# Attention rounds in another order: VectorE's steps at fixed places, the reciprocal in quarters, GpSimd's sum in two buffers

## The chip, the cores and the metric

The kernel runs on one core of one Trainium2 chip. The metric is the device time of one execution in microseconds; of the kernel before there are three runs beside the profiled one. Short names are those of the profile: PE is TensorE's matrix multiplication, PEld its loading of weights, DVE is VectorE, ACT is ScalarE, POOL is GpSimd, SP is SyncE, which issues the DMAs.

## What is computed

The reference is a trunk of two layers over 1,024 latent and 256 context tokens, each 1,024 wide. The first layer is a state-space mixer, the second an attention mixer; a last norm closes it. The change lies in the attention of the second layer alone, which computes, for 16 query heads that share 4 key heads:

```python
def attend(q, k, v):
    bsz, lq = q.shape[:2]
    q = q.reshape(bsz, lq, A_NKV, A_REP, A_HEADDIM)
    s = jnp.einsum('bqgrd,bkgd->bgrqk', q, k).astype(F32) * (A_HEADDIM ** -0.5)
    p = jax.nn.softmax(s, axis=-1).astype(v.dtype)
    o = jnp.einsum('bgrqk,bkgd->bqgrd', p, v)
    return o.reshape(bsz, lq, A_W)
...
    o_lat = (ol * jax.nn.silu(gl)) @ out_w
```

Only the latent tokens' output is wanted, over 1,280 keys (context and latent) and 1,024 queries.

## The kernel before, in words

**Units.** The attention stage works on 16 units, u = 0 to 15: a pair of heads times one half (512) of the queries. A unit goes over the ten key tiles of 128 keys, kt = 0 to 9. Its softmax needs a shift per query, and this comes from a pass of its own, the *maxima*: an approximate product of queries and keys (queries on the partitions, high parts alone), of which VectorE takes the largest along the keys. The maxima of unit u+2 are made while unit u and the beginning of u+1 are worked on.

**Rounds.** PE works in rounds, two key tiles to a round, so a unit has five (L1651 to L1682). In a round stand

- two *scores* steps, S0 and S1 (L1658 to L1664): each is 8 matmuls of three products of high and low parts and a row that adds the shift, into a pair of PSUM banks with tag "sc";
- two *maxima* steps, M0 and M1 (`maxima`, L1594 to L1622, and `max_tile`, L1457 to L1463): each is one tile of queries against 512 keys, or two against 256 (the rows with 128x256), also into a pair of "sc";
- one *values* step, V (L1674 to L1680): 4 matmuls of the two key tiles of the round before with their values, summed in the bank "ot" over the unit.

There are three pairs "sc", handed out in the order in which PE's steps stand; a step gets the pair of the step three before it, and so waits until that one has been read: a scores step by ScalarE's exponential (L1668, into a tile P), a maxima step by VectorE's maximum along the free axis (L1609).

**Sums.** The softmax's divisor is the sum of the ten P tiles. GpSimd adds tiles 0, 1, 2, 3, 5, 6 and 8 (SUM_POOL, L30), VectorE 4, 7 and 9 (`add_up`, L1635 to L1647; the first add of either takes two tiles). VectorE then joins both sums (L1688), and PE sums over the partitions, the *divisors* step D (L1698 to L1701), which ends a unit. ScalarE copies the result (L1705), VectorE takes the reciprocal (L1709), GpSimd multiplies it by the gate (L1710), VectorE multiplies the unit's output by that (L1711), into `at`. A small turn of the maxima (T, L1618) stands in the round after D.

**A block** is what lies between two D steps: five rounds of M and S and V, one T, one D. In a block, rounds 1 to 3 hold the scores of kt 4 to 9 of a unit, rounds 4 and 5 those of kt 0 to 3 of the next; all ten maxima tiles of a later unit; VectorE's adds and join of the unit; and the reciprocal, gate product and output product of the unit whose D came just before. There are 14 blocks with maxima, of which 13 have the reciprocal of a unit before them. Then two units follow without maxima.

**The order.** A planner (`Plan`, L52 to L131) lays all steps out by rank, by estimated durations and by what they need, and emits them; each engine then runs its own list strictly in that order, waiting on semaphores. PE's list is fixed: `pe` (L1579) gives every step a place, a number 5u + round + fraction, and the steps are chained in the order of these numbers (L1721). The other engines' lists come from the planner, which takes 1.3 us for an add on VectorE, 2.8 us for one on GpSimd, 3.35 us for the reciprocal.

Of the kernel before, what the change touches and what calls it, by code (L numbers as in the profile page):

```python
# [8 lines left out]
FT = mybir.dt.float32  # L9
# [3 lines left out]
OP = mybir.AluOpType  # L13
# [132 lines left out]
def emit(tc, A, out):  # L146
# [834 lines left out]
    with ExitStack() as st:  # L981
# [265 lines left out]
        tabs = []  # L1247
# [310 lines left out]
    with ExitStack() as st:  # L1558
# [7 lines left out]
            return psum("sc", [128, 2, 512])  # L1566

        NP, NU = 6, len(units)
        plan = Plan({"q": 3, "sc": 3, "ot": 1, "dn": 1, "P": NP, "accP": 1, "accV": 1, "mx": 2, "rb": 2, "sg": 2, "ob": 2, "wr": 4})
        qs3.append([S4.tile([128, 512], FR, name=f"q2{i}") for i in range(3)])  # L1570
        at = [S4.tile([128, 8, 512], FT, name=f"at{i}") for i in range(2)]
        setup = plan.op("POOL", lambda: empty_rows(qs3[2]), [], -1000, .6)
# [6 lines left out]
        def pe(when, *args, **kw):  # L1579

            turns.append((when, len(turns), plan.op("PE", *args, **kw)))
            return turns[-1][2]

        def queries(u):
            held[u] = plan.hold("q")
# [8 lines left out]
        def maxima(u):  # L1594

            x, q, R = qs3[u % 3], held[u], 100 * u - 130
            hm, t, rs = plan.hold("mx"), {}, []
            for i in range(10):
                hs = plan.hold("sc")

                def scores(i=i):
                    t[i] = pair()
                    max_tile([t[i][:, h] for h in range(2)], u, x, i)

                def reduce(i=i):
                    if not i:
                        t["m"] = max_tiles(u)
                    o = t[i].rearrange("p h (q k) -> p h q k", q=2) if i % 5 == 4 else t[i]
                    V.tensor_reduce(max_place(t["m"][0], i), o, AX.X, OP.max)  # L1609

                a = pe(5 * u - 8 + i // 2 + (.2, .4)[i % 2], scores, [brought[u]], R, .24, takes=[hs], uses=[q], table="rows")
                rs.append(plan.op("DVE", reduce, [a], R + 10 * i - 60, 1.22, takes=[] if i else [hm], uses=[hs, hm]))
            a = plan.op("DVE", lambda: largest(t["m"][1], t["m"][0]), rs, R + 30, .25, uses=[hm])
            hs = plan.hold("dn")

            def turn():
                t["p"] = psum("dn", [128, 512])[0:64, 0:128]
                T.transpose(t["p"], t["m"][1], ident)  # L1618

            a = pe(5 * u - 3 + .52, turn, [a], R, .12, takes=[hs], uses=[hm], table="cols")  # L1620
            a = plan.op("ACT", lambda: S.activation(t["m"][2], t["p"][0:8], AF.Copy), [a], R - 100, .27, uses=[hm, hs])
            shifts[u] = plan.op("SP", lambda: shift_row(x, t["m"][2]), [a], R - 100, .8, uses=[hm, q], small=True)  # L1622

        def unit(u):
            b, p = units[u]
            kv, R, t = p // 2, 100 * u, {}
            x, q = qs3[u % 3], held[u]
            ho, hg, ha = plan.hold("ot"), plan.hold("sg"), {e: plan.hold("acc" + e[0] if e == "POOL" else "accV") for e in ("POOL", "DVE")}
            sums = {"POOL": [], "DVE": []}

            def gate():
                t["g"] = S4.tile([128, 512], FT, tag="sg", bufs=2, name="sg")
                Q.dma_start(t["g"], sg_d[p, :, b * 512:(b + 1) * 512])

            def add_up(*tiles, e, rank):  # L1635

                if len(tiles) == 1:
                    return
                E, (k0, e0, h0), (kt, e1, h1), two = G if e == "POOL" else V, tiles[0], tiles[-1], len(tiles) == 2

                def add():
                    if two:
                        t[e] = S4.tile([128, 1024], FT, tag="acc" + e, bufs=1, name="acc")
                    E.tensor_tensor(t[e], t["P", k0] if two else t[e], t["P", kt], op=OP.add)  # L1644

                t["a" + e] = plan.op(e, add, [e1, e0 if two else t["a" + e]], rank, 2.8 if e == "POOL" else 1.3,
                                     takes=[ha[e]] if two else [], uses=[ha[e], h1] + ([h0] if two else []))  # L1647

            g = plan.op("SP", gate, [], R, takes=[hg])
            pv = None  # L1650
            for j in range(5):  # L1651
                kts = (2 * j, 2 * j + 1)
                hp = [plan.hold("P") for _ in kts]
                es = []
                for i, kt in enumerate(kts):
                    hs = plan.hold("sc")

                    def scores(kt=kt):  # L1658
                        o = t["s", kt] = pair()
                        k = slice(kt * 128, (kt + 1) * 128)  # L1660
                        for n in range(4):
                            for h, r in enumerate(HALF):
                                T.matmul(o[:, h], (first_row[r] if n == 3 else (kh, kl, kh)[n][r, kv, k]), x[(0, 0, 1, 2)[n]][r],  # L1663
                                         start=(n == 0), stop=(n == 3))  # L1664

                    def expo(kt=kt):
                        t["P", kt] = p_tile()
                        S.activation(t["P", kt], flat(t["s", kt]), AF.Exp)  # L1668

                    a = pe(5 * u + j + (.1, .3)[i], scores, [brought[u], shifts[u]], R, .95, takes=[hs], uses=[q], table="rows")  # L1670
                    last_scores[:] = [a]
                    es.append(plan.op("ACT", expo, [a], R + 10 * kt, 1.05, takes=[hp[i]], uses=[hs]))

                def values(kts=kts):  # L1674
                    if not kts[0]:
                        t["o"] = psum("ot", [128, 512])
                    for kt in kts:
                        for h in range(2):
                            T.matmul(t["o"][h * 64:(h + 1) * 64], vv[:, kt, kv], t["P", kt][:, h * 512:(h + 1) * 512],  # L1679
                                     start=(kt == 0), stop=(kt == NT - 1))  # L1680

                pv = pe(5 * u + j + 1.5, values, es + [pv], R, 1.72, takes=[] if j else [ho], uses=[ho] + hp, table="cols")  # L1682
                for i, kt in enumerate(kts):
                    e = "POOL" if kt in SUM_POOL else "DVE"
                    sums[e].append((kt, es[i], hp[i]))
                    add_up(*sums[e], e=e, rank=R + 10 * kt + 10)
            hd, hb, he = plan.hold("dn"), plan.hold("rb"), plan.hold("ob")
            a = plan.op("DVE", lambda: V.tensor_tensor(t["DVE"], t["DVE"], t["POOL"], op=OP.add), [t["aPOOL"], t["aDVE"]], R + 110, 1.3,  # L1688
                        uses=list(ha.values()))

            def out_of():
                t["b"] = S4.tile([128, 512], FT, tag="ob", bufs=2, name="ob")
                S.activation(t["b"], t["o"], AF.Copy)

            ev = plan.op("ACT", out_of, [pv], R + 60, .6, takes=[he], uses=[ho])


            def divisors():  # L1698
                t["d"] = psum("dn", [128, 512])
                for h in range(2):  # L1700
                    T.matmul(t["d"][h * 64:(h + 1) * 64], ones[:, 0:64], t["DVE"][:, h * 512:(h + 1) * 512], start=True, stop=True)  # L1701

            def keep():
                t["r"] = S4.tile([128, 512], FT, tag="rb", bufs=2, name="rb")
                S.activation(t["r"], t["d"], AF.Copy)  # L1705

            a = pe(5 * u + (6.6 if u < NU - 1 else 5.6), divisors, [a], R, .87, takes=[hd], uses=[ha["DVE"]], table="cols")
            a = plan.op("ACT", keep, [a], R + 30, .6, takes=[hb], uses=[hd])
            a = plan.op("DVE", lambda: V.reciprocal(t["r"], t["r"]), [a], R + 90, 3.35, uses=[hb])  # L1709
            a = plan.op("POOL", lambda: G.tensor_tensor(t["r"], t["r"], t["g"], op=OP.mult), [a, g], R + 90, 1.4, uses=[hb, hg])  # L1710
            finished[u] = plan.op("DVE", lambda: V.tensor_tensor(at[b][:, p], t["b"], t["r"], op=OP.mult), [a, ev], R + 90, .66,  # L1711
                                  uses=[hb, he])

        for u in range(NU):
            queries(u)
# [2 lines left out]
        for u in range(NU):  # L1718
            unit(u)

        turns.sort(key=lambda x: x[:2])  # L1721
        for x, y in zip(turns, turns[1:]):
            y[2].after.append(x[2])


        wparts, X4 = {}, {}
# [29 lines left out]

        def table(i, src):
            def bring():
                tabs[i] = S4.tile([128, 1024], FT, tag="acc" + ("POOL", "DVE")[i], bufs=1, name="tab")
# [140 lines left out]
```

## Time and profile before

| what | value |
|---|---|
| median of three runs | 2016.39 us (2014.74 to 2016.62) |
| profiled execution: its time, its span | 2017.43 us, 2015.7 us |
| granted TensorE clock, mean | 0.993 |
| scores steps (L1663), first and last start | 1523.0 us, 1905.4 us |
| busy over the whole span: PE, DVE, ACT, POOL | 97%, 71%, 56%, 59% |

The span runs from the first instruction to the last; the rest of a run's time lies around it. The stage that the change touches is about 387 us of it, a fifth. A share of busy time over the whole span says little here, since the state-space layer before and the output product behind it have other limits; the stage has to be looked at by its own window, and inside it by its rounds, which repeat.

### The profile page before, as it was taken

How to read it: one execution, taken by the hardware profiler on the slowest of the kernel's cores; microseconds unless marked ns; L12 is line 12 of the kernel's file. 1: busy time of each engine (PE TensorE's matmuls, PEld its weight loads, DVE VectorE, ACT ScalarE, POOL GpSimd, SP SyncE). 2: the span in 40 equal slices, each digit the busy share in tenths (PEclk: the TensorE clock that was granted, in tenths of full speed). 3: DMA queues.
4: the chain of work that ended last, by engine and by line, in shares of the span. 5: the costliest groups of instructions: out<-in, count | busy, mean ns of one | idle time of the engine just before them, and what ended most of it. 6: DMA issues, size and time to landing. Idle time of an engine off the chain costs nothing.

```text
span 2015.7 us, 30716 instructions
## 1 busy us (share of the span) xinstructions
PE 1953.1 (97%) x10728; PEld 1498.7 (74%) x10728; DVE 1433.2 (71%) x1737; ACT 1119.5 (56%) x2047; POOL 1189.5 (59%) x973
## 2 busy tenths in 40 slices
PE   8899999999999999999999999999999999999998
PEld 8778888888888788888878878887775444444476
DVE  1475897786959686866545888767675888888643
ACT  2446767666766677676734776543224445454521
POOL 1211776666846576856459787754265667776722
PEclk9989999999999999999999999999999999999999
DMA  6114463635373545455486675462233111111033
GB/s 243 63 32 119 133 188 113 187 98 163 113 198 92 150 131 162 142 142 158 147 280 215 216 252 191 156 179 93 76 91 93 32 38 48 43 43 37 6 104 105
DMA packets 163151, 255.51 MB, mean 127 GB/s; under 512 B 22490, under 2 KB 58202, under 8 KB 162996
## 3 DMA queue, kind: packets, MB, share of 16 engines
q1 hardware_dynamic: 161844, 251.71, 41.2%
q8 instruction: 84, 1.38, 0.3%
q10 hardware_dynamic: 1152, 1.84, 0.2%
q14 instruction: 71, 0.58, 0.1%
HBM read 210.78 MB, written 42.63 MB: 126 GB/s over the span
## 4 chain that ended last, share of the span: by engine, by line
PE 73%; DVE 8%; DMA 7%; POOL 3%; ACT 3%; issue 3%; SPq 2%; DVEq 0%; POOLq 0%; ACTq 0%
PE pj L168 8%; PE pj L169 7%; PE pj L170 7%; PE sc L1663 7%; PE ot L1679 7%; PE ob L168 6%; PE ob L170 6%; PE ob L169 6%; DVE acc L645 3%; PE sc L1462 2%; PE yo L837 2%; PE st L718 2%; DMA spare<-in_mod_w 2%; DMA es<-e_d 2%; PE sc L168 1%
## 5 line engine op out<-in xcount | busy, mean ns | idle before, releaser
L168 PE MATMUL pj<-inh,whi 128*128 128x512 f32 (+1 forms) x1152 | 442.0, 384 | 3.1 <-DVE dv L453 2.4
L169 PE MATMUL pj<-inl,whi 128*128 128x512 f32 (+1 forms) x1152 | 410.2, 356 | 0.8 <-POOL inl L367 0.8
L170 PE MATMUL pj<-inh,wlo 128*128 128x512 f32 (+1 forms) x1152 | 411.0, 357 | 0.0
L168 PEld LDWEIGHTS pj<-inh,whi 128*128 128x128 f32 x1152 | 219.2, 190 | 31.4 <-DVE dv L453 2.8
L170 PEld LDWEIGHTS pj<-inh,wlo 128*128 128x128 f32 x1152 | 218.5, 190 | 32.3
L645 DVE SCALAR_TENSOR_TENSOR acc<-ub,convw,acc 128x1282 f32<-128x1282 f32 x128 | 229.4, 1793 | 17.0 <-ACT acc L642 14.0
L169 PEld LDWEIGHTS pj<-inl,whi 128*128 128x128 f32 x1152 | 219.6, 191 | 26.6 <-POOL inl L367 1.2
L760 ACT ACTIVATE W<-lab,u_t 128x128 f32<-128x128 f32 x640 | 202.7, 391 | 64.6 <-POOL lab L754 42.0
L754 POOL TENSOR_SCALAR_AFFINE_SELECT lab<-lab 128x512 f32<-128x512 f32 x160 | 145.6, 915 | 153.5 <-DMA lab<-la_d 108.6
L1644 POOL TENSOR_TENSOR acc<-acc,P 128x1024 f32<-128x1024 f32 x80 | 192.8, 2411 | 64.1 <-ACT P L1668 62.6
L1668 ACT ACTIVATE P<-sc 128x1024 f32<-128x1024 f32 x160 | 162.9, 1025 | 120.0 <-PE sc L1663 104.4
L1609 DVE TENSOR_REDUCE mx<-sc 128x2 f32<-128x1024 f32 (+1 forms) x140 | 167.4, 1213 | 37.3 <-PE sc L1462 36.4
L713 POOL TENSOR_TENSOR xw<-xst,te_t 128x256 f32<-128x256 f32 x144 | 143.0, 1009 | 41.6 <-PE st L718 17.5
L1679 PE MATMUL ot<-P,vv 128*64 128x512 f32 x640 | 154.7, 605 | 0.0
L602 POOL TENSOR_TENSOR wlo<-wraw,whi 128x512 fp32r<-128x512 f32 x48 | 72.1, 1501 | 121.9 <-ACT whi L599 121.7
L1663 PE MATMUL sc<-q,kh 64*128 64x512 f32 x640 | 136.6, 423 | 4.9 <-DVE qs L1375 2.6
L1663 PEld LDWEIGHTS sc<-q,kh 64*128 64x128 f32 x640 | 60.4, 185 | 74.6 <-DVE mx L1609 29.6
L170 PE MATMUL ob<-whi,yl 128*128 128x512 f32 x288 | 113.4, 394 | 1.8 <-DVE yl L1061 1.4
L168 PE MATMUL ob<-whi,yh 128*128 128x512 f32 x288 | 113.9, 395 | 0.0
L169 PE MATMUL ob<-wlo,yh 128*128 128x512 f32 x288 | 113.0, 392 | 0.0
L902 DVE SCALAR_TENSOR_TENSOR macc<-mraw,cc,macc 128x512 f32<-128x512 f32 x98 | 101.2, 1058 | 11.1 <-DMA mraw<-in_mod_w 10.9
L732 POOL TENSOR_TENSOR tm<-PV,dec_t 128x512 f32<-128x512 f32 x64 | 92.5, 1446 | 17.8 <-DVE PV L736 16.7
(281 smaller groups left out, 4501.8 us busy)
## 6 DMA issues: line engine op xcount, KB each, us to landing
lab<-la_d SPq DMA_DIRECT2D x160, 256.0 KB
wraw<-in_w_in SPq DMA_DIRECT2D x96, 256.0 KB
workvv<-in_m_out_w SPq DMA_DIRECT2D x94, 256.0 KB
mraw<-in_mod_w SPq DMA_DIRECT2D x64, 256.0 KB
es<-e_d SPq DMA_DIRECT2D x128, 128.0 KB
wraw<-in_wqkv SPq DMA_DIRECT2D x48, 256.0 KB
spare<-in_mod_w SPq DMA_DIRECT2D x32, 256.0 KB
q_d<-qs SPq DMA_DIRECT2D x128, 64.0 KB
```

The costliest lines, as they stand in the source:

```text
L168: T.matmul(o, lh, rh, start=first, stop=False)
L169: T.matmul(o, lh, rl, start=False, stop=False)
L170: T.matmul(o, ll, rh, start=False, stop=last)
L645: V.scalar_tensor_tensor(t["a"], ub[i % 2][:, k:k + CW], convw[:, ct, k:k + 1], t["a"], op0=OP.mult, op1=OP.add)
L713: G.tensor_tensor(t[d], s["xst"][:, c], te_t[:, d, c, h4][:, :, None].to_broadcast([128, 4, 64]), op=OP.mult)
L754: G.affine_select(t["l", d], t["l", d], [[0, 4], [sgn, 128]], OP.is_ge, NEVER, base=0, channel_multiplier=-sgn)
L760: S.activation(t["w", d][:, h], t["l", d][:, h], AF.Exp, bias=u_t[:, d, c, 4 * g + h:4 * g + h + 1])
L1609: V.tensor_reduce(max_place(t["m"][0], i), o, AX.X, OP.max)
L1644: E.tensor_tensor(t[e], t["P", k0] if two else t[e], t["P", kt], op=OP.add)
L1663: T.matmul(o[:, h], (first_row[r] if n == 3 else (kh, kl, kh)[n][r, kv, k]), x[(0, 0, 1, 2)[n]][r], start=(n == 0), stop=(n == 3))
L1668: S.activation(t["P", kt], flat(t["s", kt]), AF.Exp)
L1679: T.matmul(t["o"][h * 64:(h + 1) * 64], vv[:, kt, kv], t["P", kt][:, h * 512:(h + 1) * 512], start=(kt == 0), stop=(kt == NT - 1))
```

## The change

It does four things, all in the attention stage.

1. PE's fixed places: a maxima step with even i moves from .2 to .05 of its round, ahead of the first scores step (.1). A round is M0, S0, S1, M1, V where it was S0, M0, S1, M1, V.
2. VectorE's steps get fixed places too (`dve`), in the same numbering: the maximum of M0 at .1, that of M1 at .5, an add at .75, the join at 5.7, the reciprocal's pieces at 7.3, 7.31, 7.7 and 8.3, the output product at 9.3, the last small maximum at 5u - 3.3. All of them are chained in that order.
3. The reciprocal of 128x512 becomes four of 128x128.
4. GpSimd's running sum gets two buffers instead of one (ring accP), so its first add of the next unit need not wait for VectorE's join. The two tables that later use these buffers follow suit.

```diff
-        plan = Plan({"q": 3, ..., "P": NP, "accP": 1, "accV": 1, ...})
+        plan = Plan({"q": 3, ..., "P": NP, "accP": 2, "accV": 1, ...})
...
+        steps = []
+
+        def dve(when, f, after, rank, us, **kw):
+
+            steps.append((when, len(steps), plan.op("DVE", f, after, rank, us, **kw)))
+            return steps[-1][2]
...
-                a = pe(5 * u - 8 + i // 2 + (.2, .4)[i % 2], scores, [brought[u]], R, .24, ...)
-                rs.append(plan.op("DVE", reduce, [a], R + 10 * i - 60, 1.22, ...))
+                a = pe(5 * u - 8 + i // 2 + (.05, .4)[i % 2], scores, [brought[u]], R, .24, ...)
+                rs.append(dve(5 * u - 8 + i // 2 + (.1, .5)[i % 2], reduce, [a], R + 10 * i - 60, 1.22, ...))
...
-                        t[e] = S4.tile([128, 1024], FT, tag="acc" + e, bufs=1, name="acc")
+                        t[e] = S4.tile([128, 1024], FT, tag="acc" + e, bufs={"POOL": 2, "DVE": 1}[e], name="acc")
...
+                t["a" + e] = plan.op(e, *args, **kw) if e == "POOL" else dve(5 * u + kt // 2 + .75, *args, **kw)
...
+            a = dve(5 * u + 5.7, lambda: V.tensor_tensor(t["DVE"], t["DVE"], t["POOL"], op=OP.add), ...)
...
-            a = plan.op("DVE", lambda: V.reciprocal(t["r"], t["r"]), [a], R + 90, 3.35, uses=[hb])
+            for i in range(4):
+                a = dve(5 * u + (7.3, 7.31, 7.7, 8.3)[i], lambda k=slice(i * 128, (i + 1) * 128): V.reciprocal(t["r"][:, k], t["r"][:, k]),
+                        [a], R + 90, .84, uses=[hb])
...
+            finished[u] = dve(5 * u + 9.3, lambda: V.tensor_tensor(at[b][:, p], t["b"], t["r"], op=OP.mult), ...)
...
-        turns.sort(key=lambda x: x[:2])
-        for x, y in zip(turns, turns[1:]):
-            y[2].after.append(x[2])
+        for order in (turns, steps):
+            order.sort(key=lambda x: x[:2])
+            for x, y in zip(order, order[1:]):
+                y[2].after.append(x[2])
```

**PE, from one round to the next.** In the third block, before the change: the end of S1 (its row of shifts), M1, V, then S0 of the next round in four rows, its M0, and the begin of S1. Here sc is the pair of banks, q the queries, ot the output, vv the values.

```order
L1663 MATMUL sc<-q,first_row 128x512 x2
L1462 MATMUL sc<-kh,q_15402 128x512 x2
L1679 MATMUL ot<-P,vv 64x512 x4
L1663 MATMUL sc<-q,kh 128x512 x2
L1663 MATMUL sc<-q,kl 128x512 x2
L1663 MATMUL sc<-q,kh 128x512 x2
L1663 MATMUL sc<-q,first_row 128x512 x2
L1462 MATMUL sc<-kh,q_15402 128x256 x4
L1663 MATMUL sc<-q,kh 128x512 x2
```

The same place after the change:

```order
L1672 MATMUL sc<-q,first_row 128x512 x2
L1462 MATMUL sc<-kh,q_15402 128x512 x2
L1688 MATMUL ot<-P,vv 64x512 x4
L1462 MATMUL sc<-kh,q_15402 128x256 x4
L1672 MATMUL sc<-q,kh 128x512 x2
L1672 MATMUL sc<-q,kl 128x512 x2
L1672 MATMUL sc<-q,kh 128x512 x2
L1672 MATMUL sc<-q,first_row 128x512 x2
L1672 MATMUL sc<-q,kh 128x512 x2
```

M0 (the row 128x256) has moved ahead of S0, and S1 follows S0 at once. So the pair of M0 now goes to M1 of the same round, with two scores steps between; before, M0's pair went to S0 of the next round, with S1, M1 and V between.

**VectorE, one block.** Before the change, in the middle of the stage: mx are the maxima, rb the reciprocal, at the output product, acc the sum of P tiles (acc<-P its first add, acc<-acc the join), nm the last small maximum.

```order
L1709 RECIPROCAL rb<-rb 128x512
L1609 TENSOR_REDUCE mx<-sc 128x2 x4
L1711 TENSOR_TENSOR at_15405<-ob,rb 128x512
L1644 TENSOR_TENSOR acc<-P 128x1024
L1609 TENSOR_REDUCE mx<-sc 128x2x2
L1609 TENSOR_REDUCE mx<-sc 128x2
L1644 TENSOR_TENSOR acc<-acc,P 128x1024
L1609 TENSOR_REDUCE mx<-sc 128x2
L1688 TENSOR_TENSOR acc<-acc 128x1024
L1609 TENSOR_REDUCE mx<-sc 128x2 x2
L1609 TENSOR_REDUCE mx<-sc 128x2x2
L1477 TENSOR_REDUCE nm_10308<-mx 128x8
```

After the change, the same block from its second piece of the reciprocal on (a maximum and two pieces stand before it):

```order
L1616 TENSOR_REDUCE mx<-sc 128x2
L1720 RECIPROCAL rb<-rb 128x128
L1616 TENSOR_REDUCE mx<-sc 128x2
L1720 RECIPROCAL rb<-rb 128x128
L1616 TENSOR_REDUCE mx<-sc 128x2
L1652 TENSOR_TENSOR acc<-P 128x1024
L1616 TENSOR_REDUCE mx<-sc 128x2x2
L1723 TENSOR_TENSOR at_15405<-ob,rb 128x512
L1616 TENSOR_REDUCE mx<-sc 128x2
L1652 TENSOR_TENSOR acc<-acc,P 128x1024
L1616 TENSOR_REDUCE mx<-sc 128x2 x2
L1697 TENSOR_TENSOR acc<-acc 128x1024
```

The output product has moved behind the first add and behind the maximum of round 3; each add stands right before the maximum of the next round's M0.

**GpSimd, one block.** Before the change: acc<-P is the first add of a unit, rb<-rb,sg the gate product, wol a part of the output weights.

```order
L1644 TENSOR_TENSOR acc<-P 128x1024
L1644 TENSOR_TENSOR acc<-acc,P 128x1024 x3
L1710 TENSOR_TENSOR rb<-rb,sg 128x512
L1644 TENSOR_TENSOR acc<-acc,P 128x1024
L1751 TENSOR_TENSOR wol<-wr,woh 128x512
L1644 TENSOR_TENSOR acc<-acc,P 128x1024
```

After the change:

```order
L1652 TENSOR_TENSOR acc<-P 128x1024
L1652 TENSOR_TENSOR acc<-acc,P 128x1024 x4
L1722 TENSOR_TENSOR rb<-rb,sg 128x512
L1652 TENSOR_TENSOR acc<-acc,P 128x1024
L1764 TENSOR_TENSOR wol<-wr,woh 128x512
```

The gate product now stands behind the add of kt 6 and right before that of kt 8; before, it stood ahead of the add of kt 6.

More of the change, by code (lines that the diff above doesn't have):

```diff
@@ L1568, in emit @@
         NP, NU = 6, len(units)
-        plan = Plan({"q": 3, "sc": 3, "ot": 1, "dn": 1, "P": NP, "accP": 1, "accV": 1, "mx": 2, "rb": 2, "sg": 2, "ob": 2, "wr": 4})
+        plan = Plan({"q": 3, "sc": 3, "ot": 1, "dn": 1, "P": NP, "accP": 2, "accV": 1, "mx": 2, "rb": 2, "sg": 2, "ob": 2, "wr": 4})
         qs3.append([S4.tile([128, 512], FR, name=f"q2{i}") for i in range(3)])
@@ L1609, in reduce @@
                     V.tensor_reduce(max_place(t["m"][0], i), o, AX.X, OP.max)
-                a = pe(5 * u - 8 + i // 2 + (.2, .4)[i % 2], scores, [brought[u]], R, .24, takes=[hs], uses=[q], table="rows")
-                rs.append(plan.op("DVE", reduce, [a], R + 10 * i - 60, 1.22, takes=[] if i else [hm], uses=[hs, hm]))
-            a = plan.op("DVE", lambda: largest(t["m"][1], t["m"][0]), rs, R + 30, .25, uses=[hm])
+                a = pe(5 * u - 8 + i // 2 + (.05, .4)[i % 2], scores, [brought[u]], R, .24, takes=[hs], uses=[q], table="rows")
+                rs.append(dve(5 * u - 8 + i // 2 + (.1, .5)[i % 2], reduce, [a], R + 10 * i - 60, 1.22, takes=[] if i else [hm],
+                              uses=[hs, hm]))
+            a = dve(5 * u - 3.3, lambda: largest(t["m"][1], t["m"][0]), rs, R + 30, .25, uses=[hm])
             hs = plan.hold("dn")
@@ L1642, in add @@
                     if two:
-                        t[e] = S4.tile([128, 1024], FT, tag="acc" + e, bufs=1, name="acc")
+                        t[e] = S4.tile([128, 1024], FT, tag="acc" + e, bufs={"POOL": 2, "DVE": 1}[e], name="acc")
                     E.tensor_tensor(t[e], t["P", k0] if two else t[e], t["P", kt], op=OP.add)
-                t["a" + e] = plan.op(e, add, [e1, e0 if two else t["a" + e]], rank, 2.8 if e == "POOL" else 1.3,
-                                     takes=[ha[e]] if two else [], uses=[ha[e], h1] + ([h0] if two else []))
+                args = add, [e1, e0 if two else t["a" + e]], rank, 2.8 if e == "POOL" else 1.3
+                kw = dict(takes=[ha[e]] if two else [], uses=[ha[e], h1] + ([h0] if two else []))
+                t["a" + e] = plan.op(e, *args, **kw) if e == "POOL" else dve(5 * u + kt // 2 + .75, *args, **kw)
             g = plan.op("SP", gate, [], R, takes=[hg])
@@ L1687, in unit @@
             hd, hb, he = plan.hold("dn"), plan.hold("rb"), plan.hold("ob")
-            a = plan.op("DVE", lambda: V.tensor_tensor(t["DVE"], t["DVE"], t["POOL"], op=OP.add), [t["aPOOL"], t["aDVE"]], R + 110, 1.3,
-                        uses=list(ha.values()))
+            a = dve(5 * u + 5.7, lambda: V.tensor_tensor(t["DVE"], t["DVE"], t["POOL"], op=OP.add), [t["aPOOL"], t["aDVE"]], R + 110, 1.3,
+                    uses=list(ha.values()))
             def out_of():
@@ L1708, in unit @@
             a = plan.op("ACT", keep, [a], R + 30, .6, takes=[hb], uses=[hd])
-            a = plan.op("DVE", lambda: V.reciprocal(t["r"], t["r"]), [a], R + 90, 3.35, uses=[hb])
+            for i in range(4):
+                a = dve(5 * u + (7.3, 7.31, 7.7, 8.3)[i], lambda k=slice(i * 128, (i + 1) * 128): V.reciprocal(t["r"][:, k], t["r"][:, k]),
+                        [a], R + 90, .84, uses=[hb])
             a = plan.op("POOL", lambda: G.tensor_tensor(t["r"], t["r"], t["g"], op=OP.mult), [a, g], R + 90, 1.4, uses=[hb, hg])
-            finished[u] = plan.op("DVE", lambda: V.tensor_tensor(at[b][:, p], t["b"], t["r"], op=OP.mult), [a, ev], R + 90, .66,
-                                  uses=[hb, he])
+            finished[u] = dve(5 * u + 9.3, lambda: V.tensor_tensor(at[b][:, p], t["b"], t["r"], op=OP.mult), [a, ev], R + 90, .66,
+                              uses=[hb, he])
         for u in range(NU):
@@ L1758, in bring @@
             def bring():
-                tabs[i] = S4.tile([128, 1024], FT, tag="acc" + ("POOL", "DVE")[i], bufs=1, name="tab")
+                tabs[i] = S4.tile([128, 1024], FT, tag="acc" + ("POOL", "DVE")[i], bufs=2 - i, name="tab")
                 Q.dma_start(tabs[i], rows(src, 128))
```

## Prediction

> **What bounds the kernel now.** I first read the window of the attention stage's even part, then the chain of waits inside it, round by round, then the waits and groups of VectorE and GpSimd there.
>
> ```profile
> span 2015.7 us, 30716 instructions
> ```
> ```profile
> 1600.00:1850.00 250.00, 248.29 (x1522) 121.75 (x1524) 211.10 (x164) 123.98 (x141) 174.45 (x81) 1.00 0.13 41
> ```
>
> The columns of the window's row are its length, then busy time (and instructions) of PE, PEld, DVE, ACT and POOL, the granted clock, and the DMAs' share. PE is busy for 248.3 of 250 us, VectorE for 211.1 (84%), GpSimd for 174.5 (70%), and DMAs (0.13) bound nothing: the chain should run through PE. It does:
>
> ```profile
> 1654.58 1.13 PE sc L1663 x8
> 1655.70 0.23 PE sc L1462 x2
> 1655.93 0.92 PE sc L1663 x8
> 1656.85 0.03 issue
> 1656.88 0.49 PE sc L1462 x2
> 1657.38 1.87 PE ot L1679 x8
> 1659.24 0.23 PE dn L1618
> ...
> 1662.06 0.23 PE sc L1462 x2
> 1662.29 1.87 PE ot L1679 x8
> 1664.15 1.12 PE sc L1663 x8
> 1665.28 0.23 PE sc L1462 x4
> 1665.51 0.93 PE sc L1663 x8
> 1666.44 0.02 issue
> 1666.46 0.50 PE sc L1462 x2
> 1666.96 1.87 PE ot L1679 x8
> ```
>
> Start, us, what: a round of S0, M0, S1, a short wait, M1, V. In the last five steps, 1664.15 to 1668.83, it takes 4.68 us. Two things stand out. A maxima step costs 0.23, but 0.50 when it starts after a wait; without a wait (1662.06) it is 0.23 and V follows at once. So the wait before M1 costs 0.02 + 0.27 us a round, though PE looks busy. And the first step after V costs some 0.19 more (S0 1.12 against 0.92). Who is waited for:
>
> ```profile
> PEld sc L1462 <- ACT P L1668: 20.7, 51, 0.5
> POOL acc L1644 <- DVE acc L1688: 29.0, 8, 3.9
> ```
>
> These are total, times and longest, in the same 250 us: 51 times in some 51 rounds M1 waits for the exponential that frees its pair. GpSimd's wait for VectorE's join is the one that the second buffer removes; nobody on the path waits for GpSimd there.
>
> The blocks are alike; the last V of a block's round 1, twelve blocks apart:
>
> ```profile
> 1559.31 1.87 PE ot L1679 x8
> ...
> 1853.49 1.87 PE ot L1679 x8
> ```
>
> (1853.49 - 1559.31) / 12 = 24.51 us a block. That is the quantity to forecast; 13 blocks hold a reciprocal.
>
> **PE's new order, if nobody is late.** M1 now takes the pair of M0, so it waits for VectorE instead of ScalarE. S0 takes S1's pair of the round before, long read. A round is then M0 0.23 + 0.19 (first after V), S0 and S1 0.92 each, M1 0.23, V 1.87: 4.36, or 0.32 less than 4.68. Five rounds save 1.6, and a block is 22.9 us. Over 13 or 14 blocks that is 21 to 23 us of gain. It is a ceiling: M1 starts 2.26 after the end of the V before, M0 ends 0.42 after it, and VectorE's maximum has to fit between.
>
> **What VectorE needs.** Rows of it and of its neighbours in the same part:
>
> ```profile
> 1655.26 3.35 DVE L1709 RECIPROCAL rb<-rb 128x512 f32<-128x512 f32 x1 [1.93 <-ACT rb L1705]
> 1658.53 3.58 DVE L1609 TENSOR_REDUCE mx<-sc 128x2 f32<-128x1024 f32 x3
> 1662.33 1.23 DVE L1609 TENSOR_REDUCE mx<-sc 128x2 f32<-128x1024 f32 x1 [0.23 <-PE sc L1462]
> 1663.47 1.33 DVE L1711 TENSOR_TENSOR at<-ob,rb 128x512 f32<-128x512 f32 x1
> 1664.72 2.32 DVE L1644 TENSOR_TENSOR acc<-P 128x1024 f32<-128x1024 f32 x1
> ```
> ```profile
> 1661.87 2.38 POOL L1644 TENSOR_TENSOR acc<-acc,P 128x1024 f32<-128x1024 f32 x1 [0.20 <-ACT P L1668]
> 1664.19 1.76 POOL L1751 TENSOR_TENSOR wol<-wr,woh 128x512 fp32r<-128x512 f32 x1
> ```
> ```profile
> L1688 DVE TENSOR_TENSOR acc<-acc 128x1024 f32<-128x1024 f32 x10 | 12.1, 1211 | 0.2
> L1477 DVE TENSOR_REDUCE nm<-mx 128x8 f32<-128x24 f32 x11 | 2.0, 178 | 0.4
> ```
>
> A maximum takes 1.22 and the next instruction starts 1.14 after it (1662.33, 1663.47). It begins 0.04 after its maxima step's end. An undisturbed add takes 1.21 (the join, L1688).
>
> Now the rows that decide. VectorE's output product starts at 1663.47 while GpSimd adds until 1664.25; it ends at 1664.80, 0.55 after that. Its next add starts at 1664.72 while GpSimd subtracts until 1665.95; it ends at 1667.04, 1.09 after that. An operation of VectorE with two tiles in SBUF does not proceed until GpSimd's running one is done. The reciprocal (one input) and the maxima (from PSUM) are not held. GpSimd in turn: its 1.76 from 1664.19 holds VectorE's 0.55, so a VectorE operation that is already waiting goes first. The opposite case, where GpSimd's next operation is queued and VectorE still waits for a result of GpSimd's:
>
> ```profile
> 1922.95 1.74 POOL L1710 TENSOR_TENSOR rb<-rb,sg 128x512 f32<-128x512 f32 x1
> 1924.65 1.29 POOL L1751 TENSOR_TENSOR klw<-wr,khw 128x512 fp32r<-128x512 f32 x1
> ```
> ```profile
> 1924.72 1.77 DVE L1711 TENSOR_TENSOR at<-ob,rb 128x512 f32<-128x512 f32 x1 [1.18 <-POOL rb L1710]
> ```
>
> The gate product ends at 1924.69, GpSimd's next starts at once, and the output product (1924.72) waits until 1925.94 and ends 0.55 later. After the change the output product stands in just this situation, with an add of 2.37 behind the gate product.
>
> **A block laid out by these rows** (us from the end of the D before; R is a piece of the reciprocal, mx the maximum of the step named). A quarter: 3.35 is 0.15 fixed (the 0.178 of nm less its 24 elements at 1.14 us per 1,024) and 3.20 for 512 columns, so 0.95, and the next starts 0.87 after it. Bounds: 0.84 (a plain quarter) to 1.02 (0.84 and a whole nm). ScalarE's times:
>
> ```profile
> 1654.62 0.60 ACT L1705 ACTIVATE rb<-dn 128x512 f32<-128x512 f32 x1 [2.18 <-PE dn L1701]
> 1655.80 2.11 ACT L1668 ACTIVATE P<-sc 128x1024 f32<-128x1024 f32 x2 [0.58 <-PE sc L1663]
> ```
> ```profile
> 1658.06 2.37 POOL L1644 TENSOR_TENSOR acc<-acc,P 128x1024 f32<-128x1024 f32 x1 [1.80 <-ACT P L1668]
> ```
>
> An exponential starts 0.10 after its scores end (1655.70), two take 2.11, and GpSimd's add starts 0.15 after its tile (1657.91).
>
> - Round 1 (0 to 4.36): mx M0 0.47 to 1.69, in time for M1 at 2.26. R 1.61, R 2.48, mx M1 3.35, R 4.49.
> - Round 2 (T, then 4.59 to 8.95): mx M0 5.36 to 6.58; M1 at 6.85 is safe by 0.2. R 6.50, mx M1 7.37, and the add of kt 4 and 7 asks at 8.51. GpSimd took kt 6 at 7.20 and holds it until 9.57. So the add ends at 10.65.
> - Round 3 (from 8.95): mx M0 only 10.57 to 11.79. M1, due at 11.21, starts at 11.85: 0.64 late, and 0.27 for starting after a wait. V ends at 14.22. The gate product, held by that add, ends at 11.80; kt 8 follows from 11.76 to 14.13. The output product asks at 11.8, ends at 14.68. Then mx M1 14.60 to 15.82, the add of kt 9 to 16.95, and the next mx.
> - Round 4 (from 14.22): S1, due at 15.56, needs M1's pair and starts at 15.88, 0.32 late and 0.2 for the new start. mx M0 16.87 to 18.09, so M1, due at 17.00, starts at 18.15: 1.15 late, and 0.27. V ends at 20.52. The second buffer lets GpSimd's first add of the next unit start when its tiles are there, 18.28 to 20.65; the join, asking at 19.84, ends at 21.73. Before, GpSimd waited for the join.
> - Round 5 (from 20.52): mx M0 21.65 to 22.87; M1, due at 22.78, 0.15 late and 0.27. V ends at 25.30, D (0.86) at 26.16.
>
> The lateness adds up to 0.91 + 0.52 + 1.42 + 0.42 = 3.27, on 22.9: 26.16, which is 1.65 us more than 24.51. The next block begins with VectorE idle, so it repeats. The first block has no reciprocal; there the join asks within 0.1 us of GpSimd's add, so it may gain or lose 1.3, taken as nothing. Units without maxima: the quarters' extra 0.2 lies under PE's other work. SP's loads move by a row; at a DMA share of 0.13 they cost nothing.
>
> **Sum.** 13 x 1.65 = +21.4 us, made against the span of 2015.7 (the profiled execution took 2017.4 in all, the median of three runs is 2016.4). Put on the median: **2038 us**.
>
> [...]
>
> **Rivals.**
>
> *VectorE keeps up* (no add is ever held). Speaks for it: the join took 1.21 in every block before. Against: the first add took 2.32 above. Every block 22.9: 14 x -1.6, 1994 us. 7%.
>
> *Only kt 6 holds an add*: the output product gets in ahead of kt 8, and the join ahead of GpSimd's first add. Round 3 loses 0.91, a block is 23.8; 14 x -0.7, 2006 us. The point is whether VectorE sees the gate product's end before GpSimd takes up kt 8; the rows at 1924.7 say no. 14%. Something between this and my forecast, about as before: 5%.
>
> *The output product first, the rest held.* It ends at 12.45, mx M1 at 13.62; kt 8 runs to 14.65 and holds the add of kt 9 until 15.73; M1 of round 4 is 0.45 late and the join still loses (18.6 against 17.8), which makes M1 of round 5 0.85 late. Block 25.6, +1.1: 2031 us. 14%.
>
> *PE's clock falls in the new pauses.* In the stage it is granted in full (1.00). After a pause of 2.38 us it was not:
>
> ```profile
> 1912.38 0.50 PE L170 MATMUL sc<-woh,P 128*128 128x512 f32 x1 [2.38 <-DVE P L1778]
> ```
> ```profile
> 1910.00:1920.00 10.00, 6.68 (x17) 3.78 (x17) 10.00 (x8) 3.15 (x6) 3.47 (x2) 0.67 0.35 121
> ```
>
> If 1.47 us of pause in round 4 did the same, up to 10.00 - 6.68 = 3.3 us a block would come on top: 2081 us. 5%. [...]
>
> **How the numbers follow.** My layout as it stands has 50%, other waits on top of it 5%. Slower: 50 + 14 + 5 + 5 = 74%; the same within 0.2% (4 us, about what a measurement of this kernel can tell): 5%; faster 21%. The likeliest alone spans 2031 to 2045 (a block 0.5 us shorter or longer, for the quarters' bounds and who gets in first). The range for 8 in 10 reaches from below the kt 6 case to there, 2004 to 2045, and leaves out the full gain and the clock.
>
> **What would show it.** Right: a block of about 26.2; M1 of rounds 3 and 4 waiting for DVE mx; the output product over 2 us long; the join near 1.9; GpSimd no longer waiting for the join; ScalarE's release of M1 gone. Wrong: adds of 1.21 throughout, blocks under 24.5, or no PE waits for DVE mx over 0.5 us.

## The result and the profile after

| what | before | after |
|---|---|---|
| median | 2015.97 us (4 runs, 2014.74 to 2016.62) | 2038.60 us (4 runs, 2037.39 to 2040.09) |
| ratio after to before, 95% interval | | 1.0109 (1.0093 to 1.0124) |
| profiled execution: its time, its span | 2017.43, 2015.7 us | 2038.81, 2037.1 us |

The changed kernel is 1.1% slower. First the same window of the attention stage as before; its columns are length, then busy time (and instructions) of PE, PEld, DVE, ACT and POOL, granted clock, DMA share and GB/s:

```profile
1600.00:1850.00 250.00, 231.08 (x1424) 114.39 (x1426) 218.91 (x183) 111.11 (x133) 170.20 (x75) 0.99 0.12 38
```

PE was busy for 248.3 of these 250 us and now for 231.1: it waits openly, though its order was meant for fewer waits. The waits say for whom (us in total, times, longest):

```profile
PEld sc L1462 <- DVE mx L1616: 29.3, 28, 1.5
...
PE sc L1462 <- DVE mx L1616: 16.8, 19, 1.1
...
PEld sc L1672 <- DVE mx L1616: 6.4, 9, 0.7
```

Of the other engines PE waits for VectorE alone, for its maxima: 28 times before an M1 (three times a block), nine times before an S1 (once a block). The waits for ScalarE's exponential are gone from this list, and so is GpSimd's wait for the join. Now the begin and the end of the run of D steps in the chain, and the two that lie around its one odd block:

```profile
1555.10 0.86 PE dn L1710 x4
1581.16 0.86 PE dn L1710 x4
...
1659.41 0.86 PE dn L1710 x4
1686.82 0.86 PE dn L1710 x4
1712.89 0.86 PE dn L1710 x4
...
1895.58 0.86 PE dn L1710 x4
```

A block takes 26.06 us (1581.16 - 1555.10; eleven of the 13 lie between 26.04 and 26.09), one takes 26.35, and one 27.41 (1686.82 - 1659.41). All 13 take 340.48 us, or 26.19 each against 24.51.

Here is why. VectorE, from the last piece of the reciprocal to the end of a block (start, us, line, operation):

```profile
1693.97 0.93 DVE L1720 RECIPROCAL rb<-rb 128x128 f32<-128x128 f32 x1
1694.82 1.21 DVE L1616 TENSOR_REDUCE mx<-sc 128x2 f32<-128x1024 f32 x1
1695.94 2.40 DVE L1652 TENSOR_TENSOR acc<-P 128x1024 f32<-128x1024 f32 x1
1698.28 1.21 DVE L1616 TENSOR_REDUCE mx<-sc 128x4 f32<-128x1024 f32 x1
1699.52 2.83 DVE L1723 TENSOR_TENSOR at<-ob,rb 128x512 f32<-128x512 f32 x1
1702.28 1.21 DVE L1616 TENSOR_REDUCE mx<-sc 128x2 f32<-128x1024 f32 x1
1703.41 1.21 DVE L1652 TENSOR_TENSOR acc<-acc,P 128x1024 f32<-128x1024 f32 x1
1704.55 1.22 DVE L1616 TENSOR_REDUCE mx<-sc 128x2 f32<-128x1024 f32 x1
1706.36 1.23 DVE L1616 TENSOR_REDUCE mx<-sc 128x2 f32<-128x1024 f32 x1 [0.60 <-PE sc L1462]
1707.50 1.82 DVE L1697 TENSOR_TENSOR acc<-acc 128x1024 f32<-128x1024 f32 x1
1709.25 1.21 DVE L1616 TENSOR_REDUCE mx<-sc 128x2 f32<-128x1024 f32 x1
```

GpSimd in the same time:

```profile
1694.90 2.37 POOL L1652 TENSOR_TENSOR acc<-acc,P 128x1024 f32<-128x1024 f32 x1 [1.31 <-ACT P L1677]
1697.22 2.27 POOL L1722 TENSOR_TENSOR rb<-rb,sg 128x512 f32<-128x512 f32 x1
1699.45 2.36 POOL L1652 TENSOR_TENSOR acc<-acc,P 128x1024 f32<-128x1024 f32 x1
1701.77 1.73 POOL L1764 TENSOR_TENSOR wol<-wr,woh 128x512 fp32r<-128x512 f32 x1
1705.88 2.36 POOL L1652 TENSOR_TENSOR acc<-P 128x1024 f32<-128x1024 f32 x1 [2.39 <-ACT P L1677]
```

Read the two together; an operation asks when its turn has come and its inputs are there. The first add asks at 1695.94, 1.04 after GpSimd began kt 6; that ends at 1697.27, and the add 1.07 later. The gate product waits in its turn and ends at 1699.49. GpSimd begins kt 8 at 1699.45 and VectorE the output product at 1699.52: VectorE is 0.07 us too late, and the output product takes 2.83 (undisturbed it takes 0.68, experiment 4), until 0.54 after the end of kt 8 at 1701.81. The join (1707.50) meets GpSimd's first add of the next unit and ends 1.08 after it. Only the add of kt 9 (1703.41) is undisturbed. Behind each held operation stands a maximum, and for it PE waits:

```profile
1699.54 0.50 PE L1462 MATMUL sc<-kh,q 64*128 64x512 f32 x2 [0.64 <-DVE mx L1616]
...
1703.55 0.50 PE L1672 MATMUL sc<-q,kh 64*128 64x512 f32 x2 [0.28 <-DVE mx L1616]
...
1705.82 0.50 PE L1462 MATMUL sc<-kh,q 64*128 64x512 f32 x2 [1.07 <-DVE mx L1616]
```

These are M1 of round 3, S1 and M1 of round 4.

The sum of the profiled execution: its span grew by 21.4 us. The 13 blocks account for 21.8 of it (340.48 against 13 x 24.51). The stretch from the stage's first scores to the first D grew by 2.0 (32.50 to 34.46 us), and those first scores began 2.5 earlier (1520.5 against 1523.0). The last item is no effect of the change: in the eleven profiled kernels told of here, whose program ahead of the stage is the same, they began anywhere from 1517.8 to 1523.0.

### The profile page after: what moved, and what is told of

Read it like the earlier page. It is cut to its first block, busy times and chain, and to the rows that moved or that the text cites. A ratio compares the mean times of both kernels' runs of the same rounds, so it can differ in the third digit from the quotient of the medians.

```text
span 2037.1 us, 30748 instructions
## 1 busy us (share of the span) xinstructions
PE 1946.7 (96%) x10728; PEld 1499.4 (74%) x10728; DVE 1466.5 (72%) x1785; ACT 1112.9 (55%) x2047; POOL 1200.6 (59%) x973
## 4 chain that ended last, share of the span: by engine, by line
PE 66%; DVE 13%; DMA 6%; POOL 6%; issue 5%; ACT 3%; SPq 2%; POOLq 0%; DVEq 0%; ACTq 0%
PE pj L168 7%; PE pj L169 7%; PE pj L170 7%; PE ob L168 7%; PE ob L170 7%; PE ob L169 7%; PE ot L1688 4%; DVE acc L645 3%; PE sc L1672 3%; PE yo L837 2%; DVE mx L1616 2%; PE st L718 2%; DMA es<-e_d 2%; DMA spare<-in_mod_w 2%; POOL acc L1652 2%
## 5 line engine op out<-in xcount | busy, mean ns | idle before, releaser
L1677 ACT ACTIVATE P<-sc 128x1024 f32<-128x1024 f32 x160 | 156.6, 1023 | 138.9 <-PE sc L1672 128.5
L1672 PE MATMUL sc<-q,kh 64*128 64x512 f32 x640 | 129.3, 399 | 8.2 <-DVE mx L1616 3.6
L841 DVE TENSOR_TENSOR es<-yo,es 128x512 f32<-128x512 f32 (+1 forms) x96 | 53.1, 554 | 64.4 <-DMA es<-e_d 26.5
```

## Experiments

**Theory.** The change loses because VectorE's two-tile operations (its adds, the join and the output product, each with two inputs in SBUF) stand at places where GpSimd is adding; each is held until GpSimd's operation ends (in the rows above the first add takes 2.40, the output product 2.83 and the join 1.82 us; the undisturbed add of kt 9 takes 1.21), and a maximum that frees a pair of banks for PE stands right behind it. PE's order by itself costs nothing. **Rivals:** VectorE is simply overloaded (84% busy before, plus the quarters); PE's new order is the loss; one part, the output product or the second buffer, makes it alone.

In the tables and below, a block's length is the distance between D steps in the profiled execution. The kernels of the first four experiments ran beside the kernel before at a median of 2015.0 us, those of the next four beside 2015.29, the last beside 2012.96.

**1. Take the holds away: GpSimd's adds over 128 of their 1,024 columns.**

```diff
-                    E.tensor_tensor(t[e], t["P", k0] if two else t[e], t["P", kt], op=OP.add)
+                    n = slice(0, 128 if e == "POOL" else 1024)
+                    E.tensor_tensor(t[e][:, n], t["P", k0][:, n] if two else t[e][:, n], t["P", kt][:, n], op=OP.add)
```

(The join reads the 128 columns eight times over.)

> The changed kernel, but GpSimd adds only the first 128 of 1,024 columns of each P tile, so its adds hold nothing for long. It leaves out 7/8 of GpSimd's part of the softmax sum (and adds 1 to every divisor so that none is zero). VectorE's list, its places, the quarters, the two buffers and PE's order stay. Theory (VectorE's operations on two tiles are held by GpSimd's running add, and that is the whole loss): the adds, the output product and the join fall to about 1.2, 0.7 and 1.2 us, a block to 22.9 to 23.2 us, the time to 1994 to 2000 us. Rival (VectorE's fixed list is too long for the new rounds by itself): blocks stay above 25 us, the time at 2030 us or more.

Measured: 1994.21 us (1990.89 to 1995.79), ratio 0.9891 (0.9863 to 0.9919); blocks of 23.17. Its window, and VectorE's output product in it (count, busy, mean ns):

```profile
1600.00:1850.00 250.00, 249.39 (x1606) 129.79 (x1601) 214.39 (x206) 124.11 (x147) 60.38 (x83) 1.00 0.13 42
```
```profile
L1725 DVE TENSOR_TENSOR at<-ob,rb 128x512 f32<-128x512 f32 x11 | 7.4, 675 | 0.0
```

VectorE executes the same list in the same order, is busy for 214 of the 250 us, and PE hardly waits. The first add still takes 1.75 on the mean; that the gate product, which is whole in this run, holds it is an estimate. So VectorE is not overloaded, and PE's order is no loss when little is held: the loss is GpSimd's hold. (GpSimd also has less to do here; experiment 4 leaves its work whole.)

**2. GpSimd's sum in one buffer again** (`"accP": 1`, bufs=1; all else as changed).

> The changed kernel with GpSimd's sum in one buffer again. Theory: GpSimd waits for the join as before the change, so the join takes 1.21 us instead of 1.82, M1 of round 5 is on time, and a block loses the 0.42 us of round 5: 25.6 to 25.8 us a block, 2031 to 2034 us. Rival (the second buffer is what costs): 2016 us or less. Rival (the second buffer helps, since GpSimd starts earlier): over 2041 us.

Measured: 2032.81 us (2030.05 to 2037.99), ratio 1.0088 (1.0056 to 1.0119); blocks of 25.76. The join and M1's wait:

```profile
L1697 DVE TENSOR_TENSOR acc<-acc 128x1024 f32<-128x1024 f32 x9 | 10.9, 1215 | 0.0
```
```profile
PEld sc L1462 <- DVE mx L1616: 24.2, 19, 1.5
```

The join falls from 1.82 to 1.21, and the wait of round 5 goes (19 instead of 28). The second buffer costs 0.3 us a block here: it lets GpSimd's add run into the join.

**3. PE's order alone** (the kernel before with .05 for .2, nothing else).

> The kernel before with PE's new order alone: M0 ahead of S0, VectorE's order left to the planner, reciprocal in one piece, one buffer. In its list the output product and the first add stand one behind the other ahead of round 3's first maximum. Theory: the hold hits there too, round 3 is late by 1 us without a weight part on GpSimd and by 2 us with one, other rounds are on time: blocks of 24.4 and 25.5 us, 2018 to 2028 us. Rival (the new order of PE is sound, and only VectorE's fixed places are bad): under 2008 us. Rival (the new order of PE is the whole loss): 2035 us or more.

Measured: 2028.29 us (2022.34 to 2033.70), ratio 1.0055 (1.0030 to 1.0080), just past the upper end of the theory's range (2028), with a wide spread. The profiled execution is the slowest of the six (2033.70 us; granted clock 0.987, the others 0.989 to 0.994). Its blocks explain the time: five take 24.43 to 24.46, two take 25.57 and six 27.14 to 27.18. The eight long ones are those in which GpSimd has a weight part to do; it holds the first add (2.31 us at 1638.58, where it takes 1.21 at 1614.14 without one), and M1 of round 3 pauses for 1.70 us, elsewhere for 0.60. In six of them a stretch at half the clock follows: 3.41 us at 0.50 in the two shown here, and six of these would take 0.04 off the mean clock of the window 1600 to 1850 (6 x 3.41 x 0.5 = 10.2 of 250 us), which is 0.96 where it was 1.00 before. Windows of 3.41 us: two such pairs, and one of the two long pauses without:

```profile
1666.80:1670.21 3.41, 1.71 (x14) 0.71 (x12) 2.81 (x3) 1.89 (x2) 2.49 (x2) 1.00 0.59 187
1670.21:1673.62 3.41, 3.41 (x12) 1.09 (x10) 1.96 (x2) 0.00 (x0) 0.07 (x1) 0.50 0.13 46
1694.10:1697.52 3.42, 1.72 (x12) 0.71 (x10) 2.82 (x3) 1.77 (x2) 2.42 (x2) 0.99 0.61 151
1697.52:1700.93 3.41, 3.41 (x12) 1.08 (x9) 1.99 (x3) 0.00 (x0) 0.00 (x0) 0.50 0.21 79
1803.30:1806.70 3.40, 1.69 (x10) 0.67 (x10) 2.80 (x3) 1.18 (x2) 2.37 (x1) 1.00 0.69 216
1806.70:1810.10 3.40, 3.40 (x26) 2.06 (x24) 3.40 (x4) 1.16 (x2) 0.00 (x0) 1.00 0.04 16
```

The longer pause costs 1.1 us by itself (25.57 against 24.44), and another 1.6 when the clock halves after it. Where neither lies in a block it takes 24.43, 0.08 below before: with VectorE's steps where the planner puts them, M0 ahead of S0 gains next to nothing. The eight long blocks together take 18.6 us more than eight short ones would, and the whole span grew by 16.3 (2032.0 against 2015.7): what this execution lost is GpSimd's hold and the clock behind it.

**4. The adds behind M0's maximum.** From the trace after: kt 6, the gate product and kt 8 occupy GpSimd from 7.2 to 14.1 us of the block. The first add moves behind the maximum of round 3's M0 and the add of kt 9 behind that of round 4's, the output product behind the maximum of round 4's M0 too, the join behind that of round 5's M0.

```diff
-                t["a" + e] = plan.op(e, *args, **kw) if e == "POOL" else dve(5 * u + kt // 2 + .75, *args, **kw)
+                t["a" + e] = plan.op(e, *args, **kw) if e == "POOL" else dve(5 * u + {7: 4.2, 9: 5.25}[kt], *args, **kw)
...
-            a = dve(5 * u + 5.7, lambda: V.tensor_tensor(t["DVE"], t["DVE"], t["POOL"], op=OP.add), ...)
+            a = dve(5 * u + 6.2, lambda: V.tensor_tensor(t["DVE"], t["DVE"], t["POOL"], op=OP.add), ...)
...
-            finished[u] = dve(5 * u + 9.3, lambda: V.tensor_tensor(at[b][:, p], t["b"], t["r"], op=OP.mult), ...)
+            finished[u] = dve(5 * u + 10.2, lambda: V.tensor_tensor(at[b][:, p], t["b"], t["r"], op=OP.mult), ...)
```

> The changed kernel with three places moved, so that VectorE's two-tile operations stand behind the maximum of M0 and ahead of that of M1, where a hold of 2.4 us delays nobody: the first add in round 3, output product and second add in round 4, the join in round 5. Theory: M1 is never late, a block is 22.9 to 23.3 us, the time 1994 to 2002 us, though single operations may still be held. Rival (VectorE's list is too long for the new rounds, wherever its operations stand): 2016 us or more.

Measured: 1995.67 us (1991.10 to 1998.58), ratio 0.9898 (0.9868 to 0.9928); every block 22.94 to 22.98.

```profile
1600.00:1850.00 250.00, 250.00 (x1625) 131.34 (x1623) 217.81 (x207) 125.49 (x150) 188.84 (x85) 1.00 0.13 42
```
```profile
L1697 DVE TENSOR_TENSOR acc<-acc 128x1024 f32<-128x1024 f32 x11 | 21.4, 1949 | 0.0
L1652 DVE TENSOR_TENSOR acc<-P 128x1024 f32<-128x1024 f32 x11 | 15.1, 1376 | 0.0
...
L1723 DVE TENSOR_TENSOR at<-ob,rb 128x512 f32<-128x512 f32 x11 | 7.5, 681 | 0.0
```

PE is busy without a gap; this is the ceiling that the prediction worked out (22.9). The same engines do the same work, GpSimd's adds whole; four numbers differ. The join is still held (1.95), but no maximum that PE waits for stands behind it.

**5. The output product alone** moves from 9.3 to 10.2; adds and join stay where the change put them.

> The changed kernel with one place altered: the output product moves from 9.3 to 10.2 of the numbering, that is behind both maxima of round 4 and ahead of the join, so that GpSimd's gate product is long done when VectorE comes to it. Theory (two-tile operations of VectorE are held by GpSimd's running add, and each has to be placed by itself): the 2.83 us of the output product fall to 0.7, the pauses of PE in round 4 (0.32 and 1.15 us) go, but the first add is still held by kt 6 in round 3 and the join, now behind the output product, still meets GpSimd's first add of the next unit, so M1 of round 5 is late by some 1.8. Block 25.6 instead of 26.07: 13 x -0.47 = -6, about 2032 us (2026 to 2036). Rival (the output product's hold alone makes the loss, the rest is hidden): only round 3's 0.9 stays, block 23.9, about 2010 us.

Measured: 2033.06 us (2032.39 to 2033.61), ratio 1.0089 (1.0073 to 1.0106); blocks of 25.62, one of 25.91. The output product takes 0.68, and round 4 is nearly free of pauses; but the join:

```profile
L1697 DVE TENSOR_TENSOR acc<-acc 128x1024 f32<-128x1024 f32 x10 | 31.1, 3115 | 0.0
```

It now begins 0.36 after GpSimd's next add and is held for the rest of it; M1 of round 5 waits 1.33. The time is the theory's and not the rival's: the hold moved on. (The expectation has the output product behind both maxima of round 4; it stands between them.)

**6. PE's order of before in the changed kernel** (.2 for .05, nothing else).

> The changed kernel with PE's places of before (.2 for the even maxima step instead of .05): VectorE's fixed places, the quarters and the two buffers stay. M1 then waits for ScalarE again (0.29 us a round), but PE's next scores step needs a maxima pair only 3 us after it was filled, so that VectorE's held operations cost less. Theory: by the same rows as in the prediction a block is 25.0 us (five rounds of 4.68, T and D = 24.5, and some 0.5 from the output product's 2.83 before the maximum of round 4): 2016 to 2025 us, between the kernel before and the changed one. Rival (PE's order is a gain of 1.6 us a block whatever VectorE does): 26.07 + 1.6 = 27.7 a block, 2059 us. [...]

Measured: 2020.91 us (2016.86 to 2023.57), ratio 1.0027 (1.0017 to 1.0037); blocks of 24.91 (one of 25.09), theory 25.0. The output product (2.77) and the join (2.54) are held here too, but with PE's old order a maxima pair is wanted later: PE's matrix multiplications stand still for a maximum once a block, for 0.5 us, where in the changed kernel M1 and S1 pause for 0.64, 0.28 and 1.07.

**7. PE's order of before with the places of experiment 4.**

> The kernel with the adds and the output product behind the maxima of M0 (1995.67 us), and PE's places of before (.2 instead of .05). Theory: with VectorE never late, PE's order is worth the wait of M1 for ScalarE's exponential, 0.29 us in five rounds, and a little of the first step after V: a block is again 24.5 us, 14 x 1.55 = +22, about 2017 us (2013 to 2018). Rival (the gain lies in VectorE's places alone and PE's order is indifferent): 1994 to 1998 us.

Measured: 2037.87 us (2037.26 to 2038.47), ratio 1.0114 (1.0097 to 1.0130): both theory and rival were wrong. Eight blocks take 25.42 to 25.45, five 26.88 to 26.90. VectorE's first add and join in one of the five:

```profile
1624.09 3.30 DVE L1652 TENSOR_TENSOR acc<-P 128x1024 f32<-128x1024 f32 x1
...
1634.41 3.31 DVE L1697 TENSOR_TENSOR acc<-acc 128x1024 f32<-128x1024 f32 x1
```

GpSimd there:

```profile
1623.95 2.36 POOL L1652 TENSOR_TENSOR acc<-acc,P 128x1024 f32<-128x1024 f32 x1 [1.08 <-ACT P L1677]
...
1634.27 5.68 POOL L1652 TENSOR_TENSOR acc<-acc,P 128x1024 f32<-128x1024 f32 x2 [0.64 <-ACT P L1677]
```

And who waits on PE:

```profile
1628.58 0.50 PE L1672 MATMUL sc<-q,kh 64*128 64x512 f32 x2 [1.00 <-DVE mx L1616]
...
1637.78 1.08 PE L1710 MATMUL dn<-acc,ones 128*64 128x512 f32 x4 [1.22 <-DVE acc L1697]
```

Both lose to GpSimd by 0.14 us and are held for all of its add; S1 waits for the one, D for the other. (In the eight shorter blocks a weight part stands in GpSimd's queue ahead of that second add, and the join gets in.) The places of experiment 4 are good with the PE order in which they were found, and bad with the old one. There M0 stands behind S0, so what stands behind its maximum asks later: the first add 12.13 us into the block instead of 10.57, the join 22.45 instead of 19.32, while GpSimd's add of kt 8 begins at 11.99 instead of 11.58. The expectation took "VectorE never late" over from another PE order.

**8. The reciprocal whole, in the kernel of experiment 4.**

> The kernel with the adds and the output product behind the maxima of M0 (1995.67 us), and the reciprocal whole again, at the place of the first piece. Theory: the whole one runs from 1.7 to 5.0 us of the block, the maximum of round 1's M1 ends at 6.2 instead of 4.5, and S1 of round 2, due at 5.85, needs that pair: 0.3 late and 0.2 for the new start. Block 23.45 instead of 22.95: 13 x 0.5 = 6.5, about 2002 us (1999 to 2005). Rival (three pairs leave room enough, the quarters bring nothing): 1993 to 1997 us.

Measured: 2001.82 us (1996.44 to 2002.50), ratio 0.9926 (0.9902 to 0.9949); blocks of 23.57. The quarters are worth 0.6 us a block there, by letting maxima in between: in the run with the whole one, VectorE comes to the maximum behind it 3.26 us after the reciprocal's start (1626.38 to 1629.64), and S1 of round 2 starts (1630.86) only when that maximum has ended.

**9. One buffer, in the kernel of experiment 4.**

> The kernel with the adds and the output product behind the maxima of M0 (1995.67 us), and GpSimd's sum in one buffer again, so that its first add of the next unit waits for VectorE's join. Theory (GpSimd has time enough to come late): the join, asked for 19.4 us into the block, is then not held (1.2 instead of 2.23 us), D is not touched, GpSimd's first add starts some 20.6 instead of 16.9 us into the block and has caught up by kt 6 of the next: a block stays 22.95, 1993 to 1998 us. Rival (late adds keep the P tiles, and ScalarE and then PE wait for a free one): 0.5 us or more a block, 2002 us or more.

Measured: 1992.10 us (1989.84 to 1992.76), ratio 0.9892 (0.9866 to 0.9918); blocks of 22.95. GpSimd's wait, and the join:

```profile
POOL acc L1652 <- DVE acc L1697: 34.8, 11, 6.4
```
```profile
L1697 DVE TENSOR_TENSOR acc<-acc 128x1024 f32<-128x1024 f32 x11 | 13.4, 1215 | 0.0
```

GpSimd waits up to 6.4 us for the join, and nobody on the path notices. The second buffer brings nothing in either version. Whether this kernel is faster than that of experiment 4 the runs cannot tell; both beat the kernel before.

| PE's order | VectorE's adds and output product | block, us | time, us |
|---|---|---|---|
| S0 first | by the planner (before) | 24.51 | 2015.97 |
| M0 first | by the planner (3) | 24.43; 25.57; 27.15 | 2028.29 |
| S0 first | as changed (6) | 24.91 | 2020.91 |
| M0 first | as changed (after) | 26.06 | 2038.60 |
| S0 first | behind M0's maximum (7) | 25.44; 26.88 | 2037.87 |
| M0 first | behind M0's maximum (4) | 22.95 | 1995.67 |

M0 ahead of S0 changes a block by -0.1 us (the planner's places, undisturbed), +1.2 (the change's places) or -2.5 to -3.9 (behind M0's maximum): the parts do not add.

## Why the prediction was right

The forecast of 2038 us came out by its own mechanism, block by block. Times from the end of D (1687.68 in the rows above):

| step | predicted | measured |
|---|---|---|
| first add asks, ends | 8.51, 10.65 | 8.26, 10.66 |
| M1 of round 3 starts (waited 0.64) | 11.85 | 11.86 (0.64) |
| output product asks, ends | 11.8, 14.68 | 11.84, 14.67 |
| add of kt 9 ends | 16.95 | 16.94 |
| S1, M1 of round 4 start | 15.88, 18.15 | 15.87, 18.14 |
| join asks, ends | 19.84, 21.73 | 19.82, 21.64 |
| M1 of round 5 starts | 22.93 | 22.84 |
| block | 26.16 | 26.06 |

The first add asks 0.25 earlier than forecast, and it changes nothing: the add waits for the end of kt 6 in any case.

- **The deciding row held.** Whether the output product gets in ahead of kt 8 was read from one place of the kernel before, the rows near 1924.7. It lost, by 0.07 us, in all nine of the window (mean 2.84). The rivals "only kt 6 holds an add" and "the output product first" fell with it. Even in the old PE order of experiment 6 it took 2.77.
- **PE's order was taken as a ceiling, not as a gain.** 22.9 us a block were worked out for it, and 22.95 were reached once no maximum that PE waits for stood behind a held operation (experiment 4). "VectorE keeps up" would have been 1994; experiment 1, where it does, took 1994.2.
- **The quarters.** A piece takes 0.93 (0.95 predicted); a block's four are 1.75 for the first pair and 0.94 and 0.93, 3.62 against 3.35 whole: 0.27 more of busy time. None of it is on the path after the change, since the last piece ends at 1694.90 and kt 6 at 1697.27. Experiment 8 shows what they gain instead.
- **Mis-sized: the first block.** It was "taken as nothing", with a bound of 1.3; it cost 2.0. The join began 0.21 after GpSimd's add, was held in full (3.26), and M1 of round 5 waited 1.50 us and paid its new start (0.51 us in the chain, against 0.26 for the M1 before it). VectorE's row and GpSimd's:

```profile
1548.28 3.26 DVE L1697 TENSOR_TENSOR acc<-acc 128x1024 f32<-128x1024 f32 x1
```
```profile
1548.07 2.38 POOL L1652 TENSOR_TENSOR acc<-P 128x1024 f32<-128x1024 f32 x1 [3.75 <-ACT P L1677]
```

- **Mis-sized: the clock.** The rival had the clock fall in every block, at 5%, and the forecast in none, which was the author's estimate. It fell in one of 13 (granted clock 0.94 over that block, 1.00 over each of the others), and that block took 1.35 more. So 13 blocks cost 20.2 by their steady length (13 x 1.55, forecast 21.4), 1.35 by the clock and 0.3 by the block of 26.35. In that one GpSimd took up kt 6 later, 7.51 us into the block instead of 7.22 and 0.43 after its tile was ready instead of 0.15, so the first add was held longer (2.70 us), and M1 of round 3 waited 0.94 instead of 0.64; why GpSimd was late stays open. The first block's 2.0 and the stage's early begin (-2.5) cancel by luck: the agreement to 0.6 us is closer than the method.

## What to carry to other kernels

When operations of one engine hold up those of another, as GpSimd's adds do VectorE's here, a place in an order is good or bad by a tenth of a microsecond (0.07 and 0.14 in these traces): lay such operations of both engines out against each other, and put behind each one that may be held nothing that the critical engine waits for. A better order of one engine is worth what the others' places allow, so move them together, and read the next hold before removing one. Where an engine's queue is fixed by hand, one changed place elsewhere can make the fixed places wrong (here PE's, experiment 7 against 4).

## What the runs showed of the hardware

In experiment 3 TensorE's granted clock was 0.50 for 3.41 us, in both halved stretches quoted, right behind 3.41 us in which PE was busy for 1.71 and 1.72, half of them. The two stretches start 27.31 us apart, and the blocks there take 27.18. What makes the clock fall no run shows: in the third pair of experiment 3, 1.69 us of busy PE in 3.40 was followed by the full clock (1.00). After the change:

```profile
1675.53:1678.94 3.41, 2.06 (x16) 0.98 (x14) 2.82 (x4) 2.05 (x2) 1.02 (x2) 1.00 0.22 77
1678.94:1682.36 3.42, 3.42 (x10) 0.60 (x10) 2.96 (x2) 0.00 (x0) 1.88 (x1) 0.50 0.00 0
1702.85:1706.26 3.41, 2.06 (x16) 0.88 (x12) 2.91 (x3) 2.05 (x2) 1.02 (x2) 1.00 0.28 77
1706.26:1709.68 3.42, 3.42 (x24) 1.79 (x24) 3.32 (x3) 0.64 (x2) 1.98 (x1) 1.00 0.00 0
```

The same 2.06 us of busy PE was followed by half the clock once (the block of 27.41) and by the full clock the next time. The halved stretches came behind pauses of PE of 1.70 us in experiment 3, and of 0.28 and 1.07 together after the change.
